# Expert-choice routing and the first gather: candidates shared four to three, expert 0's list ahead of the others', products during the gather

## The chip, the cores and the metric

One Trainium2 chip, one core. The metric is the time of one execution on the device in microseconds; the kernel before was run three times (2747.49, 2748.8 and 4392.96; the median is 2748.8). Engines are named as the profile names them: PE is TensorE (PEld its weight loads), DVE is VectorE, ACT is ScalarE, POOL is GpSimd, SP is SyncE, which here only issues DMAs.

## What is computed

One layer of a backbone over 2048 latent tokens of 1024 numbers and 256 context tokens: a mixing part (convolution and mLSTM), then a mixture of 16 SwiGLU experts, of which each picks its own 256 tokens. The change lies between the two parts. The second one, cut to what matters:

```python
def expert_choice_moe(h, w_router, w_gate, w_up, w_down):       # h: (1, 2048, 1024)
    cap = 2 * n // 16                                           # 256 tokens for each expert
    aff = softmax(einsum('nd,de->en', hs, w_router), axis=0)    # over the 16 experts
    g, idx = lax.top_k(aff, cap)                                # each expert its own list
    xe = hs[idx]
    a = einsum('ecd,edf->ecf', xe, w_gate)                      # w_gate, w_up: 16 x 1024 x 1408
    u = einsum('ecd,edf->ecf', xe, w_up)
    ye = einsum('ecf,efd->ecd', silu(a) * u, w_down) * g[..., None]
    return segment_sum(ye, idx, num_segments=n)
```

## The kernel before

The program is written with a planner that places the instructions of each engine in an order of its own and sets all waits; an engine then runs its list in that order. `tc.keep_in_program_order(instruction)` holds an instruction behind those that were written before it on its engine. All products are of fp32 split in two parts (`hi`, rounded, and `lo`, the rest), three products for one.

*The mixing part* writes each token's normalised row with its 16 affinities into `XN` in device memory (2048 rows of 1040 numbers), and a token-by-expert table of affinities into `sg` (128 partitions: 16 experts by 8 groups of tokens; 256 tokens each).

*The routing* (L896 to L994) finds for each expert the 256 highest affinities. `select` (L915 to L940) searches a threshold by counting: in each of five rounds seven candidates are compared with all keys, the first `NDV` = 5 on VectorE (L921) and the others on ScalarE (L924, a sign with a sum), the counts of the groups are added by one product (L936), and two small VectorE instructions (L937, L939) choose the next candidates. It is called twice, for the upper and the lower half of the keys. Between, POOL makes `ct` (L927) and fills the table `ix` (L934). Then L958 and L959 mark the keys above and at the threshold, POOL adds the two into `ge` (L960), two scans (L966, L967) number them, and `slot` holds for each token its place in the expert's list; it is transposed into `pt`.

*Lists of row numbers.* `hib` (L982) says which half of the list a place is in, `AH` (L983) is the place within the half for all 16 experts, and `RB` the right-hand side of the products that turn places into row numbers, made by POOL: for expert 0 (L987, L988) and for the 15 others (L993, L994). `xgather(e)` then compares `AH` of one expert with `ix` into a one-hot table `oh` (L1006), multiplies it with `RB` (16 products, L1009), copies and combines the result into `idx` (L1011, L1014), and POOL issues two indirect DMAs (L1017) that fetch 128 rows each into `gx`.

*The experts* run one after the other. `xprep(e)` transposes the gathered rows on PE (L1036) and makes `xh` on ScalarE (L1039), `xf` and `xl` on VectorE (L1041, L1042), for eight slices of 128. Then the 11 blocks of 128 hidden columns are taken in six pairs `pr`: `load_w` (L85) fetches 1 MB of gate and 1 MB of up weights into two buffers `wraw`, `split_w` rounds them on ScalarE (L92, `whi`) and subtracts on VectorE (L96, `wlo`), `wsplit_d` does the same for the down weights (L1055, L1057), and PE multiplies (L1152 to L1154; down: L1090 to L1092). A `wraw` buffer can be loaded again once both halves are made. The weights of expert 0's first pair are fetched ahead of the routing's end. Their rounding waits for `thr`, their subtraction for `idx`, through one-element copies into the target (L91, L95), which keep them out of the routing's way. Expert e + 1 is gathered after pair 1 of expert e and prepared after pair 3.

Of the kernel before, what the change touches and what calls it, by code (L numbers as in the profile page):

```python
# [8 lines left out]
F32 = mybir.dt.float32  # L9
F32R = mybir.dt.float32r  # L10
BF16 = mybir.dt.bfloat16
# [22 lines left out]
NDV = 5  # L34
# [4 lines left out]
def kernel(ctx, tc, x, c, cx, c_ctx, w_mod, b_mod, g_norm1, g_norm2, w_in, w_out, conv_w, conv_b,  # L39
# [48 lines left out]
    def split_w(raw, rows, cols, after=None, after_lo=None):  # L88
        hi = whip.tile([P, rows, cols], F32R, name="whi", tag="whi")
        if after is not None:  # L90
            S.activation(hi[:, 0, 0:1], after, AF.Copy)  # L91
        S.activation(hi, raw, AF.Copy)  # L92
        lo = whip.tile([P, rows, cols], F32R, name="wlo", tag="wlo")
        if after_lo is not None:
            V.tensor_copy(lo[:, 0, 0:1], after_lo)  # L95
        V.tensor_sub(lo, raw, hi.bitcast(F32))  # L96
        return hi, lo
# [725 lines left out]
    G.iota(jci[:, :, :, 0], pattern=[[1, 2], [2, 8]], base=0, channel_multiplier=0)  # L823
# [74 lines left out]
    RB = Cb0.rearrange("p h v -> p (h v)")[:, :NH * P].bitcast(BF16).rearrange("p (e j f) -> p e j f", e=NE, j=16)  # L898
    with tc.tile_pool(name="rt", bufs=1, reuse_waits="tile") as rt, tc.tile_pool(name="rtp", bufs=2, space=PSUM, reuse_waits="tile") as rtp:
# [60 lines left out]
        G.tensor_tensor(ge, gt, eq, op=ALU.add)  # L960
# [17 lines left out]
        for i in range(2):  # L978
            T.transpose(pt[:, i * P:(i + 1) * P], slot[:, i * P:(i + 1) * P], idb)
        hib = rt.tile([P, 2, 8, NE], BF16, name="hib")  # L980
        hibf = hib.rearrange("p a q e -> p (a q e)")
        V.tensor_scalar(hibf, pt, P + 0.5, None, op0=ALU.is_ge)  # L982
        V.scalar_tensor_tensor(AH.rearrange("p e j -> p j e"), hib.rearrange("p a q e -> p (a q) e"), -float(P),  # L983
                               pt.rearrange("p (j e) -> p j e", e=NE), op0=ALU.mult, op1=ALU.add)
        r = RB[:, 0].rearrange("p (a q) f -> p a q f", a=2)
        hb = hib[:, :, :, 0].unsqueeze(3).to_broadcast([P, 2, 8, 2])
        G.tensor_tensor(r[:, :, :, 0:2], hb, jpc, op=ALU.mult)  # L987
        G.tensor_tensor(r[:, :, :, 2:4], jpc, r[:, :, :, 0:2], op=ALU.subtract)  # L988
        for a in range(2):
            r = RB.rearrange("p e (a q) f -> p a q e f", a=2)[:, a, :, 1:]  # L990
            hb = hib[:, a, :, 1:].unsqueeze(3).to_broadcast([P, 8, NE - 1, 2])
            jb = jpc[:, a].unsqueeze(2).to_broadcast([P, 8, NE - 1, 2])
            G.tensor_tensor(r[:, :, :, 0:2], hb, jb, op=ALU.mult)  # L993
            G.tensor_tensor(r[:, :, :, 2:4], jb, r[:, :, :, 0:2], op=ALU.subtract)  # L994

    with tc.tile_pool(name="xw", bufs=2, reuse_waits="tile") as xraw, tc.tile_pool(name="xh", bufs=2, reuse_waits="tile") as xhi, \
# [5 lines left out]
        def xgather(e):  # L1002
# [3 lines left out]
            V.tensor_tensor(oh, ix, AH[:, e].unsqueeze(1).to_broadcast([P, P, 16]), op=ALU.is_equal)  # L1006
# [3 lines left out]
            ic = wk.tile([P, 4], F32, name="ic", bufs=1)  # L1010
            V.tensor_copy(ic, pi[:, 0:4])  # L1011
            idx = wk.tile([P, 2], I32, name="idx", bufs=3)
            icv = ic.rearrange("p (h f) -> p f h", f=2)
            V.scalar_tensor_tensor(idx[:, ::-1], icv[:, 0], float(P), icv[:, 1], op0=ALU.mult, op1=ALU.add)  # L1014
            gxs = [wk.tile([P, XW], F32, name="gx", bufs=2) for _ in range(2)]
            for hf_ in range(2):
                G.indirect_dma_start(out=gxs[hf_], out_offset=None, in_=XN,  # L1017
                                     in_offset=bass.IndirectOffsetOnAxis(ap=idx[:, hf_:hf_ + 1], axis=0))
            gg = wk.tile([P, 2], F32, name="gg", bufs=2)
            return gxs, gg, idx  # L1020

        def xprep(e, gth):
# [5 lines left out]
            for k2 in range(KD // 2):  # L1028
# [8 lines left out]
                for i in range(2):  # L1037
# [3 lines left out]
                    V.tensor_scalar(xf, pt[:, i], A2[:, k:k + 1], B2[:, k:k + 1], op0=ALU.mult, op1=ALU.add)  # L1041
# [83 lines left out]
        for e in range(NE):  # L1125
# [3 lines left out]
            for pr in range(npair):  # L1129
# [3 lines left out]
                for src in (w_gate_e, w_up_e):  # L1133
                    raw = load_w(src[0, e][:, f0 * P:(f0 + n) * P].rearrange("(k p) n -> p k n", p=P), KD, n * P)
                    if e == 0 and pr == 0:
                        ws.append(split_w(raw, KD, n * P, thr[:, 0:1], idx[:, 0:1]))
                    elif e == 0 and pr == 1 and not ws:
                        ws.append(split_w(raw, KD, n * P, xl.bitcast(F32)[:, 5, 0:1]))
                    else:
# [4 lines left out]
                              ml5b if e == NE - 1 else None)  # L1144
                hts = []
# [90 lines left out]
```

## Time and profile before

| | |
|---|---|
| median of three runs | 2748.8 us |
| the profiled execution | 2748.26 us |
| its span, first to last instruction | 2746.3 us |
| PE busy | 2636.5 us (96%) |
| DVE busy | 1606.5 us (58%) |
| ACT busy | 1143.5 us (42%) |
| POOL busy | 338.4 us (12%) |
| mean granted clock of PE | 0.983 |

Busy times come from the page of the profiled execution; its 40 slices show PE at 9 tenths or more in nearly all of them, at 3 in the slice that begins at 1098.5 us, with a granted clock of 6 tenths, and at 8 and 7 in the last three. A granted clock of 1.00 is 2.4 GHz and 0.50 is 1.2 GHz. In the timeline a row gives the start, the duration, the engine, the line, the operation, output and inputs with their shapes, and in brackets the idle time of the engine before it and what ended it. The durations of PE's products overlap.

### The profile page before, as it was taken

The numbers are of one execution on the slowest core, as the hardware profiler recorded it, in microseconds if no ns is written. First come the engines' busy times: TensorE is split into PE (matmuls) and PEld (weight loads), VectorE is DVE, ScalarE is ACT, GpSimd is POOL, SyncE is SP. The second block draws the span as 40 slices with busy tenths as digits, with TensorE's granted clock in tenths as the row PEclk, the third lists the DMA queues.
The fourth block names the chain that finished last, engine by engine and source line by source line (L and its number), as shares of the span: only waits on it lengthen the run. The fifth ranks groups of instructions, "written<-read, shape, count | busy, mean of one in ns | idle before, by whom it ended". The sixth has DMA issues, their size and how long they took to land. (4 is left out here: it accounts for less than half of the span.)

```text
span 2746.3 us, 42864 instructions
## 1 busy us (share of the span) xinstructions
PE 2636.5 (96%) x17550; PEld 2376.2 (87%) x17550; DVE 1606.5 (58%) x2603; ACT 1143.5 (42%) x1682; POOL 338.4 (12%) x351
## 2 busy tenths in 40 slices
PE   8999999999999999399999999999999999999887
PEld 5988888888878888289999999999999999999877
DVE  5356445544566566656556656655665565566584
ACT  3243333423534443244444444444444444444443
POOL 1010000000111111300011001101100110110253
PEclk9999999999999999699999999999999999999989
DMA  8444545635665654076666666766766675676765
GB/s 267 135 151 150 181 150 163 190 116 159 206 211 181 203 192 147 35 242 204 198 205 215 193 206 202 218 197 192 223 196 197 212 220 181 205 225 193 264 236 183
DMA packets 382534, 524.57 MB, mean 191 GB/s; under 512 B 15073, under 2 KB 322737, under 8 KB 380289
## 3 DMA queue, kind: packets, MB, share of 16 engines
q1 hardware_dynamic: 327968, 437.96, 49.5%
q10 hardware_dynamic: 43792, 46.55, 5.0%
q0 software_dynamic: 10576, 37.32, 4.9%
q8 instruction: 137, 2.24, 0.3%
q14 instruction: 61, 0.49, 0.1%
HBM read 449.05 MB, written 72.61 MB: 190 GB/s over the span
## 5 line engine op out<-in xcount | busy, mean ns | idle before, releaser
L1154 PE MATMUL psx<-xh,wlo 128*128 128x256 f32 x2816 | 788.6, 280 | 1.1 <-DVE wlo L96 1.1
L1152 PE MATMUL psx<-xh,whi 128*128 128x256 f32 x2816 | 789.1, 281 | 0.0
L1153 PE MATMUL psx<-xl,whi 128*128 128x256 f32 x2816 | 786.4, 280 | 2.3 <-DVE xl L1042 2.3
L96 DVE TENSOR_TENSOR wlo<-wraw,whi 128x2048 fp32r<-128x2048 f32 x248 | 539.3, 2185 | 315.6 <-ACT whi L92 315.3
L92 ACT ACTIVATE whi<-wraw 128x2048 fp32r<-128x2048 f32 x248 | 445.8, 1803 | 361.6 <-PE psx L1153 114.9
L1153 PEld LDWEIGHTS psx<-xl,whi 128*128 128x128 f32 x2816 | 530.8, 189 | 5.5 <-DVE xl L1042 3.0
L1154 PEld LDWEIGHTS psx<-xh,wlo 128*128 128x128 f32 x2816 | 530.8, 189 | 1.9 <-DVE wlo L96 1.8
L1152 PEld LDWEIGHTS psx<-xh,whi 128*128 128x128 f32 x2816 | 529.8, 189 | 2.5
L1092 PE MATMUL ac<-dhi,hl 128*128 128x512 f32 x704 | 278.4, 397 | 4.3 <-DVE hl L1161 4.3
L1090 PE MATMUL ac<-dhi,hh 128*128 128x512 f32 x704 | 280.9, 399 | 0.0
L1091 PE MATMUL ac<-dlo,hh 128*128 128x512 f32 x704 | 279.2, 397 | 0.0
L1057 DVE TENSOR_TENSOR dlo<-draw,dhi 128x2048 fp32r<-128x2048 f32 x96 | 202.6, 2111 | 111.9 <-ACT dhi L1055 111.9
L417 PE MATMUL ps<-hlo,whi 128*128 128x512 f32 (+1 forms) x672 | 259.4, 387 | 0.0
L418 PE MATMUL ps<-hhi,wlo 128*128 128x512 f32 (+1 forms) x672 | 258.9, 386 | 0.0
L416 PE MATMUL ps<-hhi,whi 128*128 128x512 f32 (+1 forms) x672 | 258.4, 387 | 0.0
L1114 POOL DMA_INDIRECT ACC<-yv,idx x28 | 82.2, 2937 | 1134.2 <-DVE yv L1109 1021.0
L1055 ACT ACTIVATE dhi<-draw 128x2048 fp32r<-128x2048 f32 x96 | 169.9, 1771 | 72.5 <-PE ac L1092 72.4
L1159 ACT ACTIVATE hh<-sgt 128x256 fp32r<-128x256 f32 x176 | 73.2, 417 | 299.6 <-DVE sgt L1157 299.6
L1092 PEld LDWEIGHTS ac<-dhi,hl 128*128 128x128 f32 x704 | 132.7, 189 | 36.6 <-DVE hl L1161 4.6
L1156 ACT ACTIVATE sgt<-psx 128x256 f32<-128x256 f32 x176 | 65.6, 374 | 224.0 <-PE psx L1154 224.0
L1090 PEld LDWEIGHTS ac<-dhi,hh 128*128 128x128 f32 x704 | 133.1, 189 | 27.2
L1091 PEld LDWEIGHTS ac<-dlo,hh 128*128 128x128 f32 x704 | 133.1, 189 | 27.2
(405 smaller groups left out, 3978.7 us busy)
## 6 DMA issues: line engine op xcount, KB each, us to landing
wraw<-in_w_gate_e_dram SPq DMA_DIRECT2D x80, 1024.0 KB, 6.3
wraw<-in_w_up_e_dram SPq DMA_DIRECT2D x80, 1024.0 KB, 5.5
draw<-in_w_down_e_dram SPq DMA_DIRECT2D x80, 1024.0 KB, 5.3
wraw<-in_w_in_dram SPq DMA_DIRECT2D x56, 1024.0 KB, 5.5
pk<-PK SPq DMA_DIRECT2D x16, 1284.0 KB, 7.7
xt<-in_x_dram SPq DMA_DIRECT2D x32, 512.0 KB, 5.1
wraw<-in_w_mod_dram SPq DMA_DIRECT2D x16, 1024.0 KB, 6.9
wm<-in_w_mod_dram SPq DMA_DIRECT2D x8, 1024.0 KB, 12.0
```

Of the source, the lines that this page charges most:

```text
L92: S.activation(hi, raw, AF.Copy)
L96: V.tensor_sub(lo, raw, hi.bitcast(F32))
L416: T.matmul(ps[:, :ntok], wh, his[k], start=k == 0, stop=False)
L417: T.matmul(ps[:, :ntok], wh, los[k], start=False, stop=False)
L418: T.matmul(ps[:, :ntok], lo[:, k, i * P:(i + 1) * P], his[k], start=False, stop=k == KD - 1)
L1057: V.tensor_sub(lo, raw, hi.bitcast(F32))
L1090: T.matmul(ac, hhs, dh[:, i, sl], start=f == 0, stop=False)
L1091: T.matmul(ac, hhs, dl[:, i, sl], start=False, stop=False)
L1092: T.matmul(ac, hls, dh[:, i, sl], start=False, stop=f == NFT - 1)
L1152: T.matmul(ps[:, m_], wh, xh[:, k], start=k == 0, stop=False)
L1153: T.matmul(ps[:, m_], wh, xl[:, k], start=False, stop=False)
L1154: T.matmul(ps[:, m_], lo[:, k, i * P:(i + 1) * P], xh[:, k], start=False, stop=k == KD - 1)
```

## The change

VectorE counts four candidates in a round and ScalarE three. `ge` is one comparison on VectorE. Only expert 0's places are made at first, its `RB` products run on VectorE, and its one-hot is made in two halves; ScalarE keeps a copy of the transposed places in `slt_`. The row numbers come from one reduction, for which the first number of each token pair holds multiples of 128. Behind the first gather's issue stand twenty products whose result nobody reads. The first pair's `lo` subtractions wait for a POOL instruction that is kept behind both gather instructions, and no longer for `idx` itself. Places and `RB` of the other 15 experts follow once expert 0's `xl` is made. In expert 0's preparation every second `xf` is ScalarE's.

```diff
-NDV = 5
+NDV = 4
         if after_lo is not None:
-            V.tensor_copy(lo[:, 0, 0:1], after_lo)
+            tc.keep_in_program_order(G.tensor_copy(lo[:, 0, 0:1], after_lo))
         V.tensor_sub(lo, raw, hi.bitcast(F32))
...
-    G.iota(jci[:, :, :, 0], pattern=[[1, 2], [2, 8]], base=0, channel_multiplier=0)
+    G.iota(jci[:, :, :, 0], pattern=[[P, 2], [2 * P, 8]], base=0, channel_multiplier=0)
...
+    hib = ghb[:, 0:P].bitcast(BF16).rearrange("p (a q e) -> p a q e", a=2, e=NE)
+    slt_ = ghb[:, P:2 * P].bitcast(BF16)
+
+    def slot_places(src, es):
+        n = es.stop - es.start
+        return V.scalar_tensor_tensor(AH[:, es].rearrange("p e j -> p j e"), hib.rearrange("p a q e -> p (a q) e")[:, :, es],
+                                      -float(P), src.rearrange("p (j e) -> p j e", e=NE)[:, :, es], op0=ALU.mult, op1=ALU.add)
...
-        G.tensor_tensor(ge, gt, eq, op=ALU.add)
+        V.tensor_scalar(ge, key, kt, None, op0=ALU.is_ge)
...
-        V.tensor_scalar(hibf, pt, P + 0.5, None, op0=ALU.is_ge)
-        V.scalar_tensor_tensor(AH.rearrange("p e j -> p j e"), hib.rearrange("p a q e -> p (a q) e"), -float(P),
-                               pt.rearrange("p (j e) -> p j e", e=NE), op0=ALU.mult, op1=ALU.add)
+        V.tensor_scalar(hib.rearrange("p a q e -> p (a q e)"), pt, P + 0.5, None, op0=ALU.is_ge)
+        slot_places(pt, slice(0, 1))
         r = RB[:, 0].rearrange("p (a q) f -> p a q f", a=2)
         hb = hib[:, :, :, 0].unsqueeze(3).to_broadcast([P, 2, 8, 2])
-        G.tensor_tensor(r[:, :, :, 0:2], hb, jpc, op=ALU.mult)
-        G.tensor_tensor(r[:, :, :, 2:4], jpc, r[:, :, :, 0:2], op=ALU.subtract)
-        for a in range(2):
-            ...
+        V.tensor_tensor(r[:, :, :, 0:2], hb, jpc, op=ALU.mult)
+        V.tensor_tensor(r[:, :, :, 2:4], jpc, r[:, :, :, 0:2], op=ALU.subtract)
+        S.activation(slt_, pt, AF.Copy)
...
-            V.tensor_tensor(oh, ix, AH[:, e].unsqueeze(1).to_broadcast([P, P, 16]), op=ALU.is_equal)
+            for js in ((slice(0, 8), slice(8, 16)) if e == 0 else (slice(0, 16),)):
+                n = js.stop - js.start
+                V.tensor_tensor(oh[:, :, js], ix[:, :, js], AH[:, e, js].unsqueeze(1).to_broadcast([P, P, n]),
+                                op=ALU.is_equal)
...
-            ic = wk.tile([P, 4], F32, name="ic", bufs=1)
-            V.tensor_copy(ic, pi[:, 0:4])
             idx = wk.tile([P, 2], I32, name="idx", bufs=3)
-            icv = ic.rearrange("p (h f) -> p f h", f=2)
-            V.scalar_tensor_tensor(idx[:, ::-1], icv[:, 0], float(P), icv[:, 1], op0=ALU.mult, op1=ALU.add)
+            with nc.allow_low_precision(reason="whole numbers up to 2047"):
+                V.tensor_reduce(idx[:, ::-1], pi[:, 0:4].rearrange("p (h f) -> p h f", f=2), axis=AX.X, op=ALU.add)
...
+            if e == 0:
+                warm = pmm.tile([P, 512], F32, name="warm", tag="mm")
+                for j in range(20):
+                    tc.keep_in_program_order(T.matmul(warm, oh[:, :, j % 16], ix[:, 0:32].rearrange("p a j -> p (a j)"),
+                                                      start=True, stop=True))
...
+        def other_places(behind):
+            tc.keep_in_program_order(G.tensor_copy(RB[:, 1, 0, 0:1], behind))
+            tc.keep_in_program_order(slot_places(slt_, slice(1, NE)))
+            for a in range(2):
+                r = RB.rearrange("p e (a q) f -> p a q e f", a=2)[:, a, :, 1:]
+                hb = hib[:, a, :, 1:].unsqueeze(3).to_broadcast([P, 8, NE - 1, 2])
+                jb = jpc[:, a].unsqueeze(2).to_broadcast([P, 8, NE - 1, 2])
+                tc.keep_in_program_order(G.tensor_tensor(r[:, :, :, 0:2], hb, jb, op=ALU.mult))
+                G.tensor_tensor(r[:, :, :, 2:4], jb, r[:, :, :, 0:2], op=ALU.subtract)
...
-                    V.tensor_scalar(xf, pt[:, i], A2[:, k:k + 1], B2[:, k:k + 1], op0=ALU.mult, op1=ALU.add)
+                    if e == 0 and i:
+                        S.activation(xf, pt[:, i], AF.Identity, scale=A2[:, k:k + 1], bias=B2[:, k:k + 1])
+                    else:
+                        V.tensor_scalar(xf, pt[:, i], A2[:, k:k + 1], B2[:, k:k + 1], op0=ALU.mult, op1=ALU.add)
...
-                        ws.append(split_w(raw, KD, n * P, thr[:, 0:1], idx[:, 0:1]))
+                        ws.append(split_w(raw, KD, n * P, thr[:, 0:1], nhalf))
...
+                if e == 0 and pr == 0:
+                    other_places(xl.bitcast(F32)[:, KD - 1, 0:1])
```

## Rows read from the trace of the kernel before

**Rows 1.** Stages: start and end, length, busy us of PE, PEld, DVE, ACT, POOL; clock, DMA, GB/s.

```profile
1120.00:1152.00 32.00, 1.90 (x12) 1.03 (x10) 26.68 (x137) 10.94 (x40) 9.14 (x29) 0.50 0.04 17
...
1174.00:1182.00 8.00, 7.64 (x47) 7.13 (x48) 6.28 (x18) 4.45 (x10) 0.00 (x0) 0.79 0.84 305
1182.00:1200.00 18.00, 18.00 (x156) 17.65 (x156) 15.90 (x16) 11.98 (x12) 1.28 (x2) 1.00 0.68 237
1200.00:2500.00 1300.00, 1300.00 (x9407) 1213.82 (x9406) 779.86 (x880) 593.41 (x655) 119.69 (x53) 1.00 0.65 204
```

**Rows 2.** Timeline of one round of the search (start, us, engine, line, operation).

```profile
1127.20 0.51 ACT L924 ACTIVATE jk<-ghb,cand 128x256 bf16<-128x256 int16 x1 [1.89 <-DVE cand L939]
...
1128.11 0.19 ACT L924 ACTIVATION_READ_ACCUMULATOR jk<-ghb,cand 128x1 bf16 x1
...
1128.75 0.09 DVE L921 DVE_READ_ACCUMULATOR jk<-ghb,cand 128x1 bf16 x1
...
1129.15 0.09 DVE L921 DVE_READ_ACCUMULATOR jk<-ghb,cand 128x1 bf16 x1
```

**Rows 3.** Timeline from the scans to expert 0's row numbers.

```profile
1153.27 0.69 DVE L966 TENSOR_TENSOR_SCAN sc<-gt,zz 128x256 bf16<-128x256 bf16 x1
...
1153.44 0.98 POOL L960 TENSOR_TENSOR ge<-gt,eq 128x256 bf16<-128x256 bf16 x1 [3.68 <-DVE eq L959]
1153.87 1.09 DVE L967 TENSOR_TENSOR_SCAN sc<-eq,zz 128x256 bf16<-128x256 bf16 x1
...
1157.55 0.29 DVE L982 TENSOR_SCALAR hib<-pt 128x256 bf16<-128x256 bf16 x1 [0.49 <-PE pt L979]
1157.88 1.24 DVE L983 SCALAR_TENSOR_TENSOR UA<-hib,pt 128x256 bf16<-128x256 bf16 x1
...
1159.15 1.22 DVE L1006 TENSOR_TENSOR oh<-ix,UA 128x2048 bf16<-128x2048 bf16 x1
...
1160.53 1.09 PE L1009 MATMUL pi<-Cb,oh 128*128 128x4 bf16 x16 [3.02 <-POOL Cb L988]
1161.67 0.16 DVE L1011 COPY ic<-pi 128x4 f32<-128x4 f32 x1 [1.29 <-PE pi L1009]
1161.86 0.16 DVE L1014 SCALAR_TENSOR_TENSOR idx<-ic 128x2 int32<-128x2 f32 x1
```

**Rows 4.** Timeline of expert 0's gather, its landing and VectorE beside it.

```profile
1162.32 4.49 DVE L96 TENSOR_TENSOR wlo<-wraw,whi 128x2048 fp32r<-128x2048 f32 x2
1162.90 2.71 POOL L1017 DMA_INDIRECT gx<-XN,idx  x1 [1.32 <-issue]
...
1165.91 1.73 POOL L1017 DMA_INDIRECT gx<-XN,idx  x1 [0.30 <-issue]
...
1174.17 0.15 DVE L1025 COPY gg<-gx 128x1 f32<-128x1 f32 x1 [2.51 <-DMA gx<-XN,idx]
```

**Rows 5.** Timeline: gather instructions of experts 1 and 2, VectorE beside the latter.

```profile
1198.41 0.94 POOL L1017 DMA_INDIRECT gx<-XN,idx  x1 [30.77 <-DVE hl L1161]
...
1304.48 2.29 DVE L1057 TENSOR_TENSOR dlo<-draw,dhi 128x2048 fp32r<-128x2048 f32 x1
...
1305.34 2.30 POOL L1017 DMA_INDIRECT gx<-XN,idx  x1 [6.01 <-issue]
```

**Rows 6.** All 32 gather instructions, L1017: from issue to landing.

```profile
DMA to landing us min/median/max: 6.5/8.0/9.9
```

**Rows 7.** Timeline of expert 0's preparation: transposes, first products, first and last slices.

```profile
1174.19 2.82 PE L1036 MATMUL ac<-ident,gx 128*128 128x128 f32 x12 [1.54 <-DMA gx<-XN,idx]
...
1175.78 0.54 DVE L1041 TENSOR_SCALAR xf<-ac,A,B 128x256 f32<-128x256 f32 x1 [1.33 <-ACT xh L1039]
...
1176.67 0.78 PE L1152 MATMUL psx<-xh,whi 128*128 128x256 f32 x2
...
1182.43 0.42 DVE L1042 TENSOR_TENSOR xl<-xf,xh 128x256 fp32r<-128x256 f32 x1
```

**Rows 8.** The page's DMA issues: gate weights, KB each, median us to landing.

```profile
wraw<-in_w_gate_e_dram SPq DMA_DIRECT2D x80, 1024.0 KB, 6.3
```

More of the change, by code (lines that the diff above doesn't have):

```diff
@@ L979 @@
             T.transpose(pt[:, i * P:(i + 1) * P], slot[:, i * P:(i + 1) * P], idb)
-        hib = rt.tile([P, 2, 8, NE], BF16, name="hib")
-        hibf = hib.rearrange("p a q e -> p (a q e)")
-        V.tensor_scalar(hibf, pt, P + 0.5, None, op0=ALU.is_ge)
-        V.scalar_tensor_tensor(AH.rearrange("p e j -> p j e"), hib.rearrange("p a q e -> p (a q) e"), -float(P),
-                               pt.rearrange("p (j e) -> p j e", e=NE), op0=ALU.mult, op1=ALU.add)
+        V.tensor_scalar(hib.rearrange("p a q e -> p (a q e)"), pt, P + 0.5, None, op0=ALU.is_ge)
+        slot_places(pt, slice(0, 1))
         r = RB[:, 0].rearrange("p (a q) f -> p a q f", a=2)
         hb = hib[:, :, :, 0].unsqueeze(3).to_broadcast([P, 2, 8, 2])
-        G.tensor_tensor(r[:, :, :, 0:2], hb, jpc, op=ALU.mult)
-        G.tensor_tensor(r[:, :, :, 2:4], jpc, r[:, :, :, 0:2], op=ALU.subtract)
-        for a in range(2):
[L990 to L994, printed above, removed]
+        V.tensor_tensor(r[:, :, :, 0:2], hb, jpc, op=ALU.mult)
+        V.tensor_tensor(r[:, :, :, 2:4], jpc, r[:, :, :, 0:2], op=ALU.subtract)
+        S.activation(slt_, pt, AF.Copy)
     with tc.tile_pool(name="xw", bufs=2, reuse_waits="tile") as xraw, tc.tile_pool(name="xh", bufs=2, reuse_waits="tile") as xhi, \
```

## The prediction

> **What bounds the kernel now.** Read the busy time by stage first [rows 1]. From 1200 to 2500 us TensorE is busy in every microsecond (1300.00 of 1300.00) at the full granted clock, and so it is from 1182 to 1200. Ahead of that lies a stage in which it does almost nothing: from 1120 to 1152 it is busy 1.90 of 32 us at 0.50 of its clock, and VectorE 26.68. This is the routing; its result, the row numbers of expert 0, starts the first gather, and the gather starts the experts. So the stage from 1120 to 1182 is a chain, and a microsecond taken out of it moves everything behind it, as long as the weights keep up. I write T0 for the end of the instruction that gives expert 0's row numbers, 1162.02 [rows 3].
>
> The rest of the chain was read from the timeline, in order of time: one round of the search [rows 2], the end of the routing [rows 3], the gather and what VectorE does meanwhile [rows 4], the same POOL instruction later on [rows 5, 6], and the preparation of expert 0's tokens [rows 7].
>
> **The search, L917 to L939 (part a).** A round counts five candidates on VectorE and two on ScalarE. The count reads follow each other by 0.40 us (1128.75, 1129.15), the fifth ends at 1129.24, and TensorE waits for it. ScalarE begins at 1127.20, and its second read is over at 1128.30 [rows 2]. With four and three, VectorE ends at 1128.84. ScalarE's third candidate adds one activation, 0.51, so its third read ends at 1128.81: a tie, with the limit left where it is. Two calls of five rounds: 10 x 0.40 = 4.0. A tie leaves TensorE waiting for two engines instead of one, for which I take off 0.1 in all; if ScalarE's hand-over cost 0.1 in each round, 3.0 would be left. I take **3.9** (3.0 to 4.0).
>
> **`ge` (part b).** POOL's addition, 0.98, leaves the list and a comparison of 256 elements joins VectorE's, which is back to back there. The nearest row is L982, 0.29. What may come back: the second of two equal scans, which ran beside POOL's addition for longer, shows 1.09 where the first shows 0.69 [rows 3]. If POOL was the cause, 0.40 - 0.25 = 0.15 is won, if not 0.25 is lost. I take **0.15** (-0.25 to 0.3).
>
> **Places and one-hot of expert 0 (part c).** Before: L982 begins at 1157.55, the places of all 16 experts take 1.24, the one-hot 1.22 and ends at 1160.37; the 16 products follow and the copy that reads them can start 1.3 later, at 1161.67 (T0 less 0.35). After, on VectorE: L982 0.33 with its gap; places of one expert, 16 elements, 0.25; two small products 0.2 each, which POOL did beside the one-hot; two half one-hots, each half of 1.14 and a fixed part of 0.08, so 0.65. That is 2.28 instead of 2.82. Behind it only the second eight products are left: 1.09 / 2 + 0.2 = 0.75 instead of 1.3. Sum 0.54 + 0.55 = **1.1**. If the shorter inner run of 8 halved the one-hot's rate, 1.2 would be lost (-0.1 to 1.3). **Row numbers (part d):** two instructions of 0.16 and 0.16 with gaps, 0.35, become one: **0.2**.
>
> **The gather (part e).** POOL's first gather instruction took 2.71 and the second 1.73, while VectorE ran two `lo` subtractions, 4.49, from 1162.32 [rows 4]. For expert 1, with VectorE free, it took 0.94. For expert 2 it took 2.30: VectorE was in a subtraction of the same form from 1304.48 to 1306.77, and POOL ended 0.87 after that [rows 5]. In [rows 4] too both end about 0.9 after a subtraction. So the issue waits for VectorE's subtraction, and the change puts these behind POOL's marker, which stands behind both issues. The two issues then take 0.94 each instead of 2.71 and 1.73: the second begins at T0 + 0.88 + 0.94 + 0.30 = T0 + 2.1 and not T0 + 3.9, and the first `lo` ends, and lets SP load the next weights, no sooner than T0 + 5.5 (it did at T0 + 2.6). The flight from issue to data was 8.3 (1165.91 to 1174.17), against those weights; the shortest of 32 is 6.5 [rows 6]. I take 6.5, since no weights move for most of it: landing at T0 + 8.6 instead of T0 + 12.15, **3.6** (1.8 with 8.3; the 0.4 that remain to 4.0 if it is shorter than any seen).
>
> The Trainium skill's page "SBUF — State Buffer", section "Who interferes with whom", says that a tensor_tensor with two SBUF inputs takes only the read half of the port pair that it shares with GpSimd, and that its probe did not see one stall a DMA issued there. By it the moved subtractions free nothing of the issue, 2.6 us of the sum are gone, and the time would be 2740.8. The rows of experts 1 and 2 speak against it; it is the second rival below.
>
> The moved work stays hidden: the two `lo` run from T0 + 3.3 to T0 + 7.8, under the flight, and are first read after the landing. If the landing came before T0 + 7, they would hold the preparation back by what they overlap.
>
> **Products during the gather and preparation of tokens (part f).** TensorE's clock was at its lower level when the tokens came, and rose 3.2 us after the twelve transposes began (from 0.50 to 1.00 between 1174 and 1182, mean 0.79). At that level twelve transposes took 2.82, and the first product began 2.5 after the landing [rows 1, 7]. The twenty products of 512 columns take 20 x 0.46 = 9.2 us if the clock stays low (156 products in 18 us at the full clock [rows 1], mostly of 256 columns: 0.115 each, times two for the columns, times two for the clock; an estimate), some 6 if it rises 3.2 after their start, as it did with the transposes. They begin at about T0 - 0.3 and end before the landing or with it. At the full clock the transposes take about 1.4, and the first product comes 1.0 earlier. Then VectorE's chain: from 1175.78 to 1182.85, 7.1 us for eight pairs of `xf` (0.54) and `xl` (0.42). Four `xf` move to ScalarE: at the 0.54 of VectorE's `xf`, the nearest row, it now has 12 x 0.54 = 6.5 and becomes the slower one, and it starts some 0.5 sooner, so the last `xl` comes about 1.2 earlier after the landing. TensorE's own holes there, some 0.5, stay. I take **1.1** (0 if the clock is low again, 2.0 if the holes go too).
>
> **Later places and products (no cost).** VectorE's places for 15 experts (about 1.2) and POOL's four products now come after expert 0's tokens. Four `xf` fewer (2.2) make room; from 1182 to 1200 VectorE has 2.1 us idle and TensorE none [rows 1]. Behind them queue expert 1's one-hot and its gather, issued at 1198.41 [rows 5], which would come 1 to 3 us later; its tokens are prepared two weight pairs on, some 33 us of TensorE's work. Without that cover it would cost 1.2.
>
> **Sum.** 3.9 + 0.15 + 1.1 + 0.2 + 3.6 + 1.1 = 10.05. The profiled execution took 2748.26 (span 2746.3 and 1.96 around it), 0.5 under the median of 2748.8. 2748.26 - 10.05 = **2738.2 us**.
>
> **Rivals.**
> - *All parts work, sizes as above*: chance 0.62, own range 2735.5 to 2742.
> - *The issue is not freed*: POOL is as slow without the subtractions; 10.05 - 2.6 = 7.5, 2740.8. Against it: 0.94 beside 2.30 [rows 5]. 0.12.
> - *The twenty products don't hold the clock* (it falls between their end and the landing, or they run over it): part f goes to zero, 2739.3. For it: no row shows the clock risen under products of this kind ahead of a wait. 0.12.
> - *More than the sum*: a flight under 6 and no holes, 12.5 won, 2735.8. 0.07.
> - *The change does not carry through* because the planner, which orders the whole program anew, loses as much among the last experts, where TensorE is not full: within 2 of 2748. 0.04.
> - *Slower than before: the next weights come too late.* They are asked for at T0 + 5.5 and not T0 + 2.6, and now meet the down weights. Their rounding on ScalarE is due 7 after the landing, T0 + 15.6, so a flight of 10 costs nothing; the median of 80 is 6.3 [rows 8]. TensorE has some 6 more before it starves, and 10 must be lost to eat the sum: it decides from a flight of 26 us, and 30 would give 2752. 0.03.
>
> **Range and chances.** The range takes in the three likeliest cases and the planner's few microseconds either way: 2733 to 2744.5. Over 2% is 55 us, about what a measurement of this kernel tells from no change; no case reaches it on either side. The routing stage from 1120 to 1174 is 54 us in all. Faster by over 2%: 0.01, within: 0.98, slower: 0.01.
>
> **What would show it.** Rounds of 2.6 and not 3.0 us; gather instructions of 0.94; both `lo` behind them; a landing 8.6 after the row numbers; the full clock at the first transposes; TensorE without holes from about 1172 on. I am wrong if a round stays at 3.0 because ScalarE ends last, if the landing stays at 12 after T0, or if TensorE waits for weights or a `lo` in the second weight pair.

## The result, and the profile after

| | before | after |
|---|---|---|
| median, same chip | 2747.5 us | 2731.7 us |
| ratio to before, 95% interval | | 0.9948 [0.9937, 0.9958] |
| profiled execution, span | 2746.3 us | 2730.7 us |
| mean granted clock of PE | 0.983 | 0.987 |

By the ratio the change gains 14.3 us (11.5 to 17.3). The medians of the table differ by 15.8; the ratio leaves out the one slow execution of the kernel before (4392.96). The sum of the prediction was 10.05, the time 2738.2 with a range down to 2733: right in direction and in being under 2%, but the median lies 1.3 us below the range (from the 2748.8 of the runs shown before, the ratio gives 2734.5, just inside). So two questions are open: did each term come out as written, and where do the other 4 us come from?

I divide both profiles at these points: the product that starts the search (S: 1119.64 and 1122.16), the row numbers of expert 0 (T0: 1162.02 and 1158.93), the landing of the second half of the gather, the first expert product, and each expert's first scatter-add into the result (the DMA that adds its rows to it).

| stretch | before | after | difference | forecast |
|---|---|---|---|---|
| start of the span to S | 1119.64 | 1122.16 | +2.52 | 0 |
| S to T0 (parts a to d) | 42.38 | 36.77 | -5.61 | -5.35 |
| T0 to the landing of the second half (e) | 12.15 | 7.03 | -5.12 | -3.6 |
| landing to first product (f) | 2.50 | 1.28 | -1.22 | -1.0 |
| first product to expert 0's first scatter (f) | 108.73 | 110.76 | +2.03 | -0.1 |
| expert 0's to expert 13's first scatter, 13 periods | 1241.70 | 1238.33 | -3.37 | 0 |
| from there to the end | 219.2 | 214.3 | -4.9 | 0 |

From S to the first scatter 9.9 are gained, almost exactly the sum, but of other parts than forecast. Then each expert takes 95.26 instead of 95.52 us, which no part of the prediction has. The last line belongs to the execution: a second profile of the unchanged kernel before has 213.6 there and one of the kernel after 215.8. The first line lies ahead of everything that the change is about. It varies too: S comes at 1119.64 to 1120.20 in the three traces of the kernel before and its variant, and at 1119.99 to 1122.80 in the eleven of the kernel after and its variants; whether some of it is the change's isn't settled.

First the stages of the kernel after (columns as in [rows 1]).

```profile
1122.00:1156.00 34.00, 3.06 (x18) 1.60 (x18) 27.56 (x136) 19.79 (x64) 9.67 (x29) 0.50 0.04 16
1156.00:1166.00 10.00, 7.82 (x40) 4.51 (x41) 5.82 (x8) 0.38 (x1) 2.42 (x4) 0.66 0.40 112
1166.00:1182.00 16.00, 15.01 (x122) 14.40 (x123) 12.10 (x22) 12.58 (x19) 4.46 (x5) 1.00 0.92 321
1182.00:1200.00 18.00, 16.62 (x123) 14.96 (x122) 12.60 (x13) 10.51 (x13) 0.00 (x0) 1.00 0.74 240
1200.00:2500.00 1300.00, 1300.00 (x9438) 1213.88 (x9438) 783.05 (x874) 598.03 (x656) 126.49 (x54) 1.00 0.65 205
```

Two things are new beside [rows 1]. From 1182 to 1200 TensorE is busy 16.62 of 18 us, where it had no hole before. And from 1166 to 1182 the DMA engines are at 0.92 with 321 GB/s: the transfers are now near their full share in that stage (0.84 and 305 from 1174 to 1182 before). From 1200 on TensorE is full as before, but in the same 1300 us there are 9438 product records instead of 9407.

**A round of the search**, timeline, to be read against [rows 2]:

```profile
1128.76 0.51 ACT L932 ACTIVATE jk<-ghb,cand 128x256 bf16<-128x256 int16 x1 [0.99 <-DVE cand L947]
...
1130.15 0.19 ACT L932 ACTIVATION_READ_ACCUMULATOR jk<-ghb,cand 128x1 bf16 x1
1130.30 0.09 DVE L929 DVE_READ_ACCUMULATOR jk<-ghb,cand 128x1 bf16 x1
...
1130.54 0.17 PE L944 MATMUL pn<-cnt,ghb 128*128 128x8 bf16 x1 [2.41 <-DVE jk L929]
```

ScalarE's third read ends at 1130.34, VectorE's fourth at 1130.39: the tie that was forecast, and VectorE still releases TensorE. From the first to the tenth choice of candidates (L937, now L945), nine rounds took 28.29 us and now take 24.70: 0.40 each.

**From the scans to the row numbers**, timeline, against [rows 3]:

```profile
1151.83 0.68 DVE L974 TENSOR_TENSOR_SCAN sc<-gt,zz 128x256 bf16<-128x256 bf16 x1
1152.43 0.67 DVE L975 TENSOR_TENSOR_SCAN sc<-eq,zz 128x256 bf16<-128x256 bf16 x1
...
1155.60 0.29 DVE L988 TENSOR_SCALAR ghb<-pt 128x256 bf16<-128x256 bf16 x1 [0.49 <-PE pt L987]
...
1156.14 1.30 DVE L1008 TENSOR_TENSOR oh<-ix,UA 128x1024 bf16<-128x1024 bf16 x2
...
1157.35 0.17 DVE L993 TENSOR_TENSOR Cb<-jpc,Cb 128x32 bf16<-128x32 bf16 x1
...
1157.58 1.16 PE L1012 MATMUL pi<-Cb,oh 128*128 128x4 bf16 x16 [2.02 <-DVE Cb L993]
1158.77 0.16 DVE L1015 TENSOR_REDUCE idx<-pi 128x2 int32<-128x4 f32 x1 [1.25 <-PE pi L1012]
```

The second scan takes 0.67 and not 1.09, now that POOL's addition no longer runs beside it. The two half one-hots take 1.30, so the shorter inner run cost nothing. But all 16 products run behind the second half and not eight of them: they wait for `Cb` L993, which the planner put behind both halves. That kept part c at 0.9 us won instead of 1.1.

**The gather**, timeline, against [rows 4] and [rows 7]:

```profile
1159.23 1.14 POOL L1018 DMA_INDIRECT gx<-XN,idx  x1 [10.71 <-DVE idx L1015]
1159.44 5.70 PE L1023 MATMUL warm<-ix,oh 128*128 128x512 bf16 x18 [0.22 <-issue]
1160.66 0.96 POOL L1018 DMA_INDIRECT gx<-XN,idx  x1 [0.30 <-issue]
1161.87 4.49 DVE L96 TENSOR_TENSOR wlo<-wraw,whi 128x2048 fp32r<-128x2048 f32 x2 [2.94 <-POOL wlo L95]
1165.96 1.53 PE L1052 MATMUL ac<-ident,gx 128*128 128x128 f32 x12 [0.38 <-DMA gx<-XN,idx]
1167.24 0.48 PE L1173 MATMUL psx<-xh,whi 128*128 128x256 f32 x2
```

Both instructions are short, the second half lands 5.3 after its issue began (8.26 before; the shortest flight of the 32 was 6.5), and the transposes run at full clock, 1.53 instead of 2.82. The trace's packet records say where the shorter flight comes from. The rows themselves move as fast as before, within 4.5 us (1161.05 to 1165.53) and 4.6 (1169.05 to 1173.64). But in the kernel before their first packet came 3.4 us after the first instruction's end, while weights moved; in the kernel after it came 0.7 after it, and the next weights' first packet only at 1165.25.

After that the gain is partly lost. TensorE's waits from 1160 to 1210 (us in total, times, longest), and ScalarE's timeline ahead of the longest:

```profile
PE psx L1173 <- ACT whi L92: 1.4, 1, 1.4
PE psx L1174 <- DVE xl L1061: 0.9, 2, 0.5
```

```profile
1176.67 1.93 ACT L1074 ACTIVATE dhi<-draw 128x2048 fp32r<-128x2048 f32 x1 [1.52 <-DMA draw<-in_w_down_e_dram]
1179.32 1.92 ACT L1074 ACTIVATE dhi<-draw 128x2048 fp32r<-128x2048 f32 x1 [0.72 <-DMA draw<-in_w_down_e_dram]
1181.26 1.28 ACT L1177 ACT_TABLE_LOAD   x1
...
1182.83 1.90 ACT L92 ACTIVATE whi<-wraw 128x2048 fp32r<-128x2048 f32 x1
```

In the kernel before, TensorE has one wait from its first expert product to expert 0's first scatter, and none for `whi`:

```profile
PE psx L1153 <- DVE xl L1042: 0.2, 1, 0.2
```

The rounding of the up weights (`whi`) stands behind the rounding of the down weights (`dhi`) on ScalarE, and that waits for its loads, 1.52 and 0.72; ScalarE's table load (the 1.28 us ahead of its first Silu) stands between, too. The loads of the down weights begin to go out 2.8 us behind the gate weights', which the moved `lo` had held to 1164.19; four megabytes at the 321 GB/s of the stage are 13 us, an estimate.

### The profile page after: what moved, and what is told of

Read it like the earlier page. It is cut to its first block, busy times and chain, and to the rows that moved or that the text cites. A ratio compares the mean times of both kernels' runs of the same rounds, so it can differ in the third digit from the quotient of the medians.

```text
span 2730.7 us, 42905 instructions
## 1 busy us (share of the span) xinstructions
PE 2635.4 (97%) x17569; PEld 2371.4 (87%) x17570; DVE 1598.7 (59%) x2566; ACT 1153.0 (42%) x1707; POOL 338.0 (12%) x351
```

## Experiments

Ratios are to the kernel before, run on the same chip. "Start" is S to expert 0's first scatter (165.8 before, 155.8 after).

| run | median | ratio | start | us per expert |
|---|---|---|---|---|
| before again (r1) | 2744.9 | 0.9998 [0.9989, 1.0007] | 165.9 | 95.52 |
| after again (r2) | 2733.3 | 0.9949 [0.9936, 0.9961] | 156.0 | 95.26 |
| after, table load early (r3) | 2741.1 | 0.9981 [0.9972, 0.9989] | 162.5 | 95.64 |
| after, `lo` beside the issue (r4) | 2732.3 | 0.9954 [0.9939, 0.9969] | 157.2 | 95.26 |
| after, tokens +96 bytes (r5) | 2745.4 | 0.9993 [0.9984, 1.0002] | 157.3 | 96.25 |
| before, tokens +96 bytes (r6) | 2761.3 | 1.0055 [1.0041, 1.0069] | 166.1 | 96.53 |
| after, tokens +128, weights +32 (r7) | 2746.8 | 1.0000 [0.9991, 1.0009] | 156.7 | 96.43 |
| after, `lo` beside, loads held (r8) | 2730.1 | 0.9939 [0.9923, 0.9954] | 155.2 | 95.26 |
| after, tokens at before's places (r9) | 2734.7 | 0.9958 [0.9945, 0.9972] | 156.0 | 95.52 |
| after, tokens +192 bytes (r10) | 2743.4 | 0.9989 [0.9980, 0.9998] | 156.8 | 96.09 |
| after, one product in the gather (r11) | 2729.7 | 0.9936 [0.9923, 0.9950] | 154.5 | 95.26 |
| after, table load in the gather (r12) | 2730.1 | 0.9936 [0.9922, 0.9949] | 156.9 | 95.26 |

**Are the 0.26 us per expert the program's or the execution's?** The two kernels again, without an edit.

> The kernel before once more, for its trace. In the two traces so far an expert's period is 95.52 us before and 95.25 after (the first scatter of experts 1 to 12), and the tail from expert 13's first scatter to the end 219.2 and 214.4. Theory A: both belong to the execution and not to the change; then this trace has a period and a tail that scatter like those two (period 95.2 to 95.5, tail 213 to 220). Theory B: they belong to the change; then 95.52 and 219 again. In either case the routing takes 41.7 us from L945's start to the row numbers and the gather lands 12.1 after them.

> The changed kernel once more, beside the former on the same chip. Theory A (the change is worth what the routing and the gather give, about 10 us, and the rest of the 16 us between the two traces was the executions'): 9 to 12 us faster than before, period and tail as the former run has them. Theory B (period and tail gain too): 14 to 16 us faster, period 95.25, tail 214. In both: routing 36.1, landing 7.0 after the row numbers, and one wait of 1.4 us of TensorE for the up weights of the second pair.

The periods came back to a hundredth, 95.52 and 95.26. They belong to the program. The tails did not: 213.6 for before here, 219.2 in the first profile. So of the two theories each had half: the period is the change's, the tail the execution's.

**The table load moved away.** One small Silu on ScalarE, in a tile of its own:

```diff
-            gg = wk.tile([P, 2], F32, name="gg", bufs=2)
-            return gxs, gg, idx
+            gg = wk.tile([P, 2], F32, name="gg", bufs=2); tab = wk.tile([P, 2], F32, name="tab", bufs=1) if e == 0 else None
+            return gxs, gg, (e == 0 and tc.keep_in_program_order(S.activation(tab[:, 0:1], nhalf, AF.Silu))) and idx or idx
```

> The changed kernel with one more ScalarE instruction, a one-element Silu whose result nobody reads, placed by the planner ahead of the search; by it the table load of 1.28 us that stood ahead of expert 0's first Silu is done there. Theory 1 (TensorE's new wait of 1.4 us for the up weights' rounding comes from ScalarE's queue, in which the table load and the Silu stand ahead of that rounding): the wait falls to 0.1 to 0.3, 1.1 to 1.3 us faster than the changed kernel. Theory 2 (the rounding waits for its buffer or for the weights themselves): the wait stays at 1.4 and the time is the same.

Some 8 us slower than after, which neither theory had. ScalarE's timeline shows the first part: the table load stands at the head of the search and waits there.

```profile
1125.02 1.28 ACT L1026 ACT_TABLE_LOAD   x1 [4.75 <-DMA XN<-xs]
...
1126.43 0.49 ACT L932 ACTIVATE jk<-ghb,cand 128x256 bf16<-128x256 int16 x1
```

The new tile lies in space that a tile of the stage before still held, so, by the wait that the row names, the activation waited for the DMA that moves that tile into `XN`, and ScalarE's first count came 3.8 us late. The wait for `whi` stayed at 1.4 without the table load, because `dhi` waited 3.06 for its loads; and in this execution the granted clock was 0.50 from 1188.57 to 1191.99, behind that wait, which the kernel after has not. And the period was 95.64, with no edit in any expert. What this kernel has in the experts and the kernel after has not is 32 bytes: the new tile pushes the split tokens `xh`, `xl` from byte 170816 of each partition to 170848, which is where they lie in the kernel before. The change had brought the shift the other way, since it needs one small tile less.

**The `lo` subtractions beside the issue again**, as before the change, on VectorE behind the row numbers:

```diff
-            tc.keep_in_program_order(G.tensor_copy(lo[:, 0, 0:1], after_lo))
+            V.tensor_copy(lo[:, 0, 0:1], after_lo)
...
-                        ws.append(split_w(raw, KD, n * P, thr[:, 0:1], nhalf))
+                        ws.append(split_w(raw, KD, n * P, thr[:, 0:1], idx[:, 0:1]))
```

> The changed kernel with the first pair's lo subtractions marked by the row numbers on VectorE again, as before, so that they run beside POOL's two gather instructions; the order of every engine is otherwise the same. Theory 1 (the subtractions hold POOL's issue and let the next weights load into the flight): gather instructions of about 2.7 and 1.7, landing 11.5 to 12.2 after the row numbers, 4 to 5 us slower than the changed kernel. Theory 2 (a tensor_tensor does not hold the issue, as the Trainium skill's page SBUF - State Buffer has it): instructions of about 1.0, landing at 7 to 9, at most 2 us slower.

The time stayed, so of the two theories neither held as a whole. Timeline:

```profile
1157.28 4.52 DVE L96 TENSOR_TENSOR wlo<-wraw,whi 128x2048 fp32r<-128x2048 f32 x2
1157.28 1.14 POOL L1018 DMA_INDIRECT gx<-XN,idx  x1 [10.71 <-DVE wlo L95]
1158.71 1.72 POOL L1018 DMA_INDIRECT gx<-XN,idx  x1 [0.30 <-issue]
...
1166.44 1.53 PE L1052 MATMUL ac<-ident,gx 128*128 128x128 f32 x12 [2.41 <-DMA gx<-XN,idx]
```

The first gather instruction starts with the first subtraction, in the same hundredth, and is not held: 1.14. The second starts inside it and ends at 1160.43, 0.9 after the subtraction's end (half of 4.52 after 1157.28). In the kernel before the first one started 0.58 into it and took 2.71 [rows 4]. So "the issue waits for the subtraction" holds for an instruction that starts inside one. The landing came 9.46 after T0 and not 7.03: 0.76 from the second instruction, the rest behind it. But the next weights were asked for 2.6 us earlier after T0 (2.65 instead of 5.26), `dhi` and `whi` had them in time, the 1.4 us wait was gone, and of 2.4 us lost 1.1 came back.

**Is the rest of that delay VectorE's or the loads'?** The same with the next gate and up loads held until the gather's second half has landed (the gate weights are asked for at 1165.04, the copy that they wait for reads that half at 1164.17):

```diff
-        raw = wrawp.tile([P, rows, cols], F32, name="wraw", tag="wraw")
+        raw = wrawp.tile([P, rows, cols], F32, name="wraw", tag="wraw"); gate is not None and V.tensor_copy(raw[:, 0, 0:1], gate)
...
-                    raw = load_w(src[0, e][:, f0 * P:(f0 + n) * P].rearrange("(k p) n -> p k n", p=P), KD, n * P)
+                    raw = load_w(src[0, e][:, f0 * P:(f0 + n) * P].rearrange("(k p) n -> p k n", p=P), KD, n * P, gg[:, 1:2] if e == 0 and pr == 1 else None)
```

> The kernel after with the two lo subtractions beside the gather's issue again, as in the run before this one of that kind, and with the loads of the next gate and up weights held back until the first half of the gather has landed, so that no weights move beside the gather. It separates the two parts of the gather's loss. There, the second gather instruction took 1.72 instead of 0.96, and from its end to the landing 5.9 passed instead of 4.3. Theory 1 (VectorE's subtraction holds the instruction that starts inside it, weights in flight slow the data): instruction 1.14 and 1.72 again, but 4.3 to 4.5 from its end to the landing, which then comes about 8 us after the row numbers (7.0 in the kernel after, 9.4 in the other run). Theory 2 (the subtractions slow the data too): 5.9 again, landing 9.4 after the row numbers. The next weights come later by some 5 us, so TensorE waits for them in the second pair in either case, by 1 to 5 us; the whole is expected at 2732 to 2738.

```profile
1157.66 4.52 DVE L96 TENSOR_TENSOR wlo<-wraw,whi 128x2048 fp32r<-128x2048 f32 x2
1157.66 1.13 POOL L1018 DMA_INDIRECT gx<-XN,idx  x1 [10.71 <-DVE wlo L95]
1159.09 1.72 POOL L1018 DMA_INDIRECT gx<-XN,idx  x1 [0.30 <-issue]
...
1164.19 1.53 PE L1052 MATMUL ac<-ident,gx 128*128 128x128 f32 x12 [0.70 <-DMA gx<-XN,idx]
```

The instructions are the same, and from the end of the second (1160.81) to the landing 3.4 pass instead of 6.0; the packets of the gather take 4.4 us from first to last instead of 7.0. Theory 1 holds in kind: the subtractions hold the instruction, weights in flight delay the data. It was off in size, since it expected 4.3 to 4.5; from its start the second half takes 5.1, about the 5.3 of the kernel after, so the subtractions cost the landing little once no weights move. The later weights then cost TensorE a wait of 1.1, so that the whole comes out about as the kernel after (2730.1, below the 2732 to 2738 expected).

**Where the tokens lie.** One line, in the kernel after and in the kernel before; orders and instructions are unchanged:

```diff
-            idx = wk.tile([P, 2], I32, name="idx", bufs=3)
+            idx = wk.tile([P, 10], I32, name="idx", bufs=3)[:, 0:2]
```

> The kernel after with one line changed: the three 8-byte tiles of row numbers are declared 40 bytes wide, of which 8 are used, so that every tile behind them, the split tokens xh and xl and the hidden values hh and hl among them, lies 96 bytes further on. No engine's order changes and no instruction. The tokens then begin 32 bytes beside a multiple of 64, as they do in the kernel before (170848) and do not in the kernel after (170816). Theory 1, that the 0.27 us per expert which the changed kernel gains in the steady part (95.25 instead of 95.52) come from where the tokens lie and not from the edits: a period of 95.5, and 15 such periods, so 4 us more than the kernel after: ratio to before 0.9963, about 2737 us, which is what the prediction's sum of 10 gives. Theory 2, that the shorter period belongs to the edits (other work in each expert's places, or the order that the planner made): the period stays at 95.25 and the time at that of the kernel after, ratio 0.9948.

> The kernel before with the same one line: row numbers' tiles 40 bytes wide, nothing else. The tokens move from 170848 to 170944, a multiple of 64. Theory 1 (where the tokens lie): the period falls from 95.52 to 95.25 and the time by 4 us, ratio to before 0.9985, with nothing of the change in the kernel. Theory 2 (the edits): the period stays at 95.52, ratio 1.0000.

That the place decides was right; that it is a matter of multiples of 64 was wrong. The first shift cost 1.0 us per expert and not 0.26. The second put before's tokens on a multiple of 64 and made it 15 us slower. From start to start, the products with the tokens take 117.4 ns in r2 and 119.4 in r5 (means over 1320 to 2500 us, worked out from the traces); 528 of them per expert, by 2.0 ns, are 1.06 us, the whole difference. The products with the down weights gain or lose nothing like it (233.3 and 232.5 ns).

```diff
-    thr = con.tile([P, 8], F32, name="thr")
+    thr = con.tile([P, 16], F32, name="thr")[:, 0:8]
```

This line beside the one above moves the weights by 32 bytes too.

> The kernel after with the row numbers' tiles 40 bytes wide and the threshold's tile 64 instead of 32 bytes wide: now the split weights (whi, wlo, dhi, dlo) and the tokens all begin at multiples of 64 (in the kernel after the tokens alone do). Order and instructions unchanged. If every operand that lies 32 bytes off costs TensorE something, as theory 1 has it for the tokens: a period under 95.25, down to about 95.0 if the weights cost as much as the tokens, and 4 us less than the kernel after, ratio 0.9934. If only the tokens matter: the period stays at 95.25 and the ratio at 0.9948. If what matters is only the place of the tokens relative to the weights: back to 95.5, ratio 0.9963.

96.43: all on multiples of 64, and 14 us slower than after. None of the three expectations held. Then the tokens exactly where the kernel before has them, by `bufs=4` instead of 3 for `idx`; and 192 bytes further on, by `[P, 18]`.

> The kernel after with a fourth 8-byte tile for the row numbers: all tokens' tiles lie 32 bytes further on, and so exactly where they lie in the kernel before (gx at 162464, xh at 170848, hh at 207712). Order and instructions unchanged. It measures the change without the shift of the tokens' tiles that it brought by needing one small tile less. Theory 1 (the tokens' place sets the products' pitch; so far 95.26 us per expert at 170816, 95.52 at 170848, 96.25 at 170912, 96.53 at 170944): a period of 95.5, first scatter as in the kernel after, so 15 x 0.26 = 4 us more than after, ratio 0.9963, 10 us under before, which is the prediction's sum. Theory 2 (the slower runs with shifted tiles were slow for another reason, their wider tiles): 95.26, ratio 0.9948.

> The kernel after with row numbers' tiles 72 bytes wide: the tokens' tiles lie 192 bytes further on, xh at 171008, a multiple of 1024, so that every slice of 256 tokens begins at one. Order and instructions unchanged. If the pitch grows with the address as it did over the four places tried (0.26 us for the first 32 bytes, 1.27 for 128): a period of 97.0 or more, 23 us more than after, ratio 1.003. If it goes in turns of 256 bytes or less: between 95.2 and 95.6, or lower, since the places tried were 64, 96, 160 and 192 past a multiple of 256 and got slower away from it: 95.0 as an estimate from 0.26 for 32 bytes, 4 us less than after, ratio 0.9934.

The first scatter-adds of experts 0 and 13 (POOL's timeline), in the kernel before, in the kernel after, in r9 and in r6:

```profile
1285.39 3.44 POOL L1114 DMA_INDIRECT ACC<-yv,idx  x1 [84.80 <-DVE yv L1109]
...
2527.10 3.41 POOL L1114 DMA_INDIRECT ACC<-yv,idx  x1 [72.31 <-DVE yv L1109]
```

```profile
1278.00 3.45 POOL L1133 DMA_INDIRECT ACC<-yv,idx  x1 [71.54 <-DVE yv L1128]
...
2516.34 3.41 POOL L1133 DMA_INDIRECT ACC<-yv,idx  x1 [73.51 <-DVE yv L1128]
```

```profile
1276.02 3.45 POOL L1133 DMA_INDIRECT ACC<-yv,idx  x1 [71.26 <-DVE yv L1128]
...
2517.72 3.41 POOL L1133 DMA_INDIRECT ACC<-yv,idx  x1 [73.63 <-DVE yv L1128]
```

```profile
1286.32 3.44 POOL L1114 DMA_INDIRECT ACC<-yv,idx  x1 [85.11 <-DVE yv L1109]
...
2541.16 3.41 POOL L1114 DMA_INDIRECT ACC<-yv,idx  x1 [73.20 <-DVE yv L1109]
```

1241.70, 1238.33, 1241.70 and 1254.84 us lie between them. The kernel after with before's places has before's period to the hundredth; the kernel before with shifted places is 13 us slower over the same 13 experts. So the steady part's gain comes from the place of the tokens' tiles and from nothing else in the change. By the offset of `xh` past a multiple of 256 bytes: 64 gives 95.26; 96 gives 95.52 (95.64 in r3, where the gathered rows lie elsewhere); 160, 96.25; 192, 96.53 (96.43 in r7, with the weights 32 bytes further on); 0, 96.09, between the two expectations. It is no ramp, since 192 bytes further on cost less than 128. Nor is the place of `xh` and `xl` alone the whole of it, since r3 and r7 differ by 0.1 from the others at their offsets. What the products meet there (other reads of the same tile, VectorE's or ScalarE's writes, the transfers) isn't settled: every run moved `xh`, `xl` and all tiles behind them together. The Trainium skill's page "SBUF — State Buffer", section "Who interferes with whom", says that TensorE never waits on anyone. The periods above differ by 1.3% with the same instructions; whether TensorE's products wait for others there, or for its own reads, no run here shows.

**The twenty products.** `range(20)` becomes `range(1)`, so nineteen are left out, which feed nothing.

> The kernel after with one product instead of twenty during the first gather. The planner orders the first two experts' work a little differently; the tokens stay at 170816. Theory 1 (the products keep the clock up, worth about 1.2 us ahead of the first expert product, as the trace shows: landing to first product 1.28 instead of 2.50): half clock until some 3 us after the landing, transposes 2.8 instead of 1.53, first product 2.5 after the landing. Theory 2, on what becomes of it: since TensorE then waits for the split tokens (0.9) and for the rounding of the up weights (1.4) after the first product in the kernel after, the later start is eaten by these waits, and the first scatter comes 0 to 1 us later than in the kernel after, counted from the start of the search; if the gain lasted, 1.2 to 2.2 later. In the whole 2731 to 2734, ratio 0.995 to 0.9957.

```profile
1165.08 2.82 PE L1052 MATMUL ac<-ident,gx 128*128 128x128 f32 x12 [1.13 <-DMA gx<-XN,idx]
...
1167.55 0.77 PE L1173 MATMUL psx<-xh,whi 128*128 128x256 f32 x2
```

The transposes are at half clock again (2.82), and the first product comes 2.47 after the landing: the products do bring 1.2 there. From it to the first scatter 108.2 us pass instead of 110.8, since TensorE waits neither for `xl` nor for `whi`. Counted from S it is 1.4 us shorter than the kernel after, against both theories. The planner also put the up weights' `whi` (1180.07) ahead of the second `dhi` (1181.87) here, so how much of the 1.4 is the products' and how much that order's stays open. The median is the lowest of all, 2729.7, but its interval overlaps that of the kernel after. So no run shows that the twenty products make the whole faster.

**The table load into the gather**, without a new tile:

```diff
-            return gxs, gg, idx
+            return gxs, gg, (e == 0 and tc.keep_in_program_order(S.activation(gg[:, 0:1], idx[:, 0:1], AF.Silu))) and idx or idx
```

> The kernel after with one small Silu activation on ScalarE that reads expert 0's row numbers, so that the table load of 1.28 us that stands at 1181.26 between the down weights' rounding and the first silu comes while ScalarE waits for the gather (it was idle for 10.0 us there). VectorE's, TensorE's and SyncE's orders are unchanged, and so are all places in memory. If the table load is what makes TensorE wait 1.4 us for the up weights' rounding, that wait falls to 0.1, the first scatter comes 1.3 us earlier from the start of the search and the time is 2730.4, ratio 0.9943. If it is the wait for the down weights ahead of it (1.52 and 0.72, and longer where the loads land later), the wait stays at about 1.4 as in the run with the table load ahead of the search, ratio 0.9948.

ScalarE's timeline and TensorE's waits:

```profile
1158.61 1.28 ACT L1026 ACT_TABLE_LOAD   x1 [2.41 <-DVE idx L1015]
...
1177.65 1.92 ACT L1074 ACTIVATE dhi<-draw 128x2048 fp32r<-128x2048 f32 x1 [2.50 <-DMA draw<-in_w_down_e_dram]
```

```profile
PE psx L1173 <- ACT whi L92: 1.0, 1, 1.0
PE psx L1174 <- DVE xl L1061: 0.9, 2, 0.5
PE psx L1173 <- DVE sgt L1178: 0.8, 1, 0.8
```

The load hides, and `dhi` now waits 2.50 instead of 1.52 for its data, which landed later in this execution: so what is left of the wait for `whi`, 1.0 of 1.4, is the down weights' loads and not the table. A new wait of 0.8 for `sgt` follows it. The first scatter came no earlier, 156.9 after S. What hiding the table load would give with the loads landing as in the kernel after isn't shown. By their ratios r8, r11 and r12 stand 2.5 to 3.3 us below the kernel after; their intervals overlap its own.

## Why the prediction was right and where it was wrong

The search, `ge` and the places were not taken out one by one; their terms are read from the traces of before and after.

- **The search, 3.9.** Right: 0.40 per round, the tie at VectorE's end (1130.34 and 1130.39). From S to the tenth choice of candidates 4.16 were gained; the 0.1 taken off for the second wait was not needed.
- **`ge`, 0.15.** 0.32. Without POOL's addition beside it the second scan fell from 1.09 to 0.67, the case that was left open.
- **Places, one-hot, row numbers, 1.3.** 1.14. The one-hot's rate held. The step that failed is "only the second eight products are left": all 16 still stood behind it, since `Cb` came last.
- **The gather, 3.6.** 5.1, above its own range of 1.8 to 4.0; this is the term that was mis-sized. The second instruction begins 1.73 after T0 instead of 3.89, which is 2.2 (forecast 1.8). The rest is the flight: taken as 6.5 because no row was shorter, it was 5.3, so 3.0 instead of 1.8. The 32 flights of [rows 6] all had weights beside them (155 KB per us or more over the 6.5 us behind each issue, by the packet records), so their minimum was no floor for a gather with none: r4 and r8 show the same gather with (6.0 from the issue's end) and without (3.4). The rival "more than the sum" had such a flight, at a chance of 0.07, but together with holes that go, and these grew.
- **The issue rival, 0.12.** It falls: 0.94 to 1.14 free, 1.72 to 2.71 when an instruction starts inside a VectorE operation on two tiles. The Trainium skill's page "SBUF — State Buffer", section "Who interferes with whom", holds that such an operation takes only the read half and stalled no issue in its probe; the instructions here end 0.8 to 1.0 after it, in all the rows shown here, so for these gathers the rows speak against it. The same section's sentence that issue order decides who blocks isn't tested by r4 and r8: there the instruction started together with the subtraction, and neither was slowed (1.14 and 1.13, and 4.52 for the two subtractions, 4.49 in the kernel after). The changed kernel shows it for the later experts too (timeline of expert 1):

```profile
1202.23 1.22 DVE L1008 TENSOR_TENSOR oh<-ix,UA 128x2048 bf16<-128x2048 bf16 x1
1202.59 1.74 POOL L1018 DMA_INDIRECT gx<-XN,idx  x1 [24.45 <-DVE idx L1015]
1203.37 2.28 DVE L1076 TENSOR_TENSOR dlo<-draw,dhi 128x2048 fp32r<-128x2048 f32 x1
1204.63 1.84 POOL L1018 DMA_INDIRECT gx<-XN,idx  x1 [0.30 <-issue]
```

  1204.33 and 1206.47 are 0.88 and 0.82 after the ends of the one-hot and of the subtraction.
- **Products and preparation, 1.1.** -0.8, below its own range of 0 to 2.0. The clock rose ahead of the transposes as forecast, the first product came 1.2 earlier, and the last `xl` too (7.4 after the landing instead of 8.7); the step that failed is "TensorE's own holes there, some 0.5, stay". An earlier start found `xl` late (0.9) and, some 16 us on, `whi` (1.4). That wait is one of the signs of being wrong that the prediction had named: TensorE waits for weights in the second pair. The slower rival had named the place, the next weights behind the moved `lo`, and priced it at nothing up to a flight of 10 us. It missed that ScalarE's queue puts the up weights behind the down weights, whose loads come at the same time.
- **The later experts, no cost.** Right for the order; wrong in taking for granted that instructions of the same form keep their pace. 15 periods of 0.26 are 3.9, and with the 9.9 from S to the first scatter that makes 13.8 of the 14.3. With before's places the change gives 0.9958, 11.5 us (7.7 to 15.1), which holds the forecast of 10.05. So it was the places that took the time out of the range. That the rest came out at the sum is in part luck: two terms off by 1.5 and 1.9 in opposite directions stand inside it.

## What to carry to other kernels

In this kernel an edit that adds or drops one small tile moves every tile behind it by 32 bytes, and the place alone is worth 4 us in the change and 15 us in r6, as much as the whole change: compare the places of the operands before a difference in a steady loop is put down to the edit, and hold them fixed when an edit is measured. A minimum over many transfers is a floor only for transfers under the same load. When a chain ahead of a full engine is shortened, ask which queue now comes late: here TensorE started 6.3 us earlier after T0, and 2.0 of that were handed back, most of it to ScalarE's order behind the next loads.

## What the hardware showed that was not expected

- The pace of a full TensorE depends on where the tokens' tiles lie: 95.26 to 96.53 us per expert for five places within 192 bytes. The two places that several runs share, 95.26 in six and 95.52 in three, repeat to 0.01.
- Multiples of 64 are not the good places: 95.26 (after) and 96.53 (r6) are both on one.
- A gather's issue is not held by a VectorE operation on two tiles that starts in the same hundredth (1.14, 1.13), and is by one that already runs (1.72 to 2.71).
- The same gather, from the end of its issue to the data: 3.4 (r8) without weights in flight, 6.0 (r4) with them beside the same instructions. Its packets take 4.4 from first to last in r8, 4.5 in the kernel after and 7.0 in r4; in the kernel before they take 4.6, but begin 3.4 after the first instruction's end, while weights move.
